# Value projection of a neighbourhood attention: every piece of side work tied to a numbered weight load

## The chip, the cores and the metric

The kernel runs on one NeuronCore of a Trainium2 chip. The metric is the device time of one execution, in microseconds (us). Five engines work side by side: TensorE (PE) multiplies matrices, VectorE (DVE) and ScalarE (ACT) work elementwise, GpSimd (POOL) does some elementwise work and issues DMAs, SyncE (SP) issues DMAs. Each takes its instructions in the order in which they were put into its program.

## The reference

One layer of a diffusion backbone over 256 latent tokens and 256 context tokens, 2048 channels each, in float32. Both are normalised and modulated to rows `h`. From `h` come the projections of a neighbourhood attention (16 heads of 64, here handled as 8 pairs of heads) and of a gated linear attention (GLA, 4 heads); both branches are gated, merged and projected out.

```python
h = _layer_norm(x) * (1.0 + scale) + shift
h_c = _layer_norm(ctx) * (1.0 + scale_c) + shift_c
aq, ak, av, az, bq, bk, bv, bz, bg, mga, mgb = _split_cols(h @ w_in[l])
y_a = _neighborhood_attention(heads(aq), heads(ak), heads(av), k_ctx, v_ctx, na_rpb[l])
y_b, y_b_c = _gla_mixer(bq, bk, bv, bg, ...)
out = _merge_branches(y_a, az, y_b, bz, mga, mgb, w_br_a[l], w_br_b[l], w_out[l])
```

A latent query attends, in one softmax, to a window of latent keys plus all context keys, with a bias table (`rpb`) on the window.

## The kernel before

All matrix products keep float32 precision by splitting each operand into a high and a low part and multiplying three times (high x high, high x low, low x high). The split of a weight is one cast on ACT (line 147, `h_...`) and one subtraction on DVE (line 149, `l_...`).

**Weight loads.** `load` (line 154) brings one unit of weights from HBM on SP's queue into a buffer `raw` (four of them), splits it into `hi` and `lo` (three of each), and the caller then multiplies with it. A weight unit is mostly 128 x 1024; in the value projection it is 128 x 704. The bias tables `rb` of the attention (line 475) use `raw` buffers too, and hold them until the scores have taken the bias. Counted from the first call of `load`: two units for the queries of each pair (`aq`, 48 matmuls of 256 columns for a pair), eight for each of the three groups of value columns (`av`, 24 matmuls of 352 columns per unit), two for the keys of pair 7 (`ak7`, 24 matmuls of 512 columns per unit), and then the GLA's keys and queries (`bk`, `bq`). The keys of pairs 0 to 6 are made earlier, in the first stage, with `h` itself.

**The order of the work.** The program text gives each instruction a place. A scheduler at compile time then puts each engine's instructions in order: among those that it expects to be ready, the earlier in the text goes first. `tc.issue_after(ins)` forces an instruction behind another one of the same engine. What the scheduler expects of durations is its own model; at run time the order is fixed, and an engine stands still at an instruction whose inputs are late.

**The stage.** The loop over `g` (line 555) projects the queries of pair 2g (`project_pair`), reads values for the pairs whose probabilities are ready (`read_values`, tile `op`), projects pair 2g+1, calls `attend` for both pairs and then `value_columns(g)`, the value projection (`va`). In the fourth round there are no value columns; `attend(6)` stands ahead of `project_pair(7)`, and the values of pair 7 are read by a hook in the GLA's first keys. `attend` works in two halves of 128 queries: scores of two heads on TensorE (tile `s`, one PSUM pair), bias and maximum on DVE (lines 485, 487), exponential on ACT (line 491), reciprocal and scaling (494 to 499), four transposes per head on TensorE (tile `tp`, line 502), copies into `pt` (506, 508). `project_pair` also splits the pair's keys (`kn`, `kl`) and moves them and parts of the queries across partitions by DMAs on POOL's queue (`kh` line 459, `q` line 470).

**The rows.** The GLA later reads `h` with tokens on the partitions. Since `h` was made transposed, eight blocks of rows are computed anew and stored in HBM (`hrows`). For a block n, `fetch_rows` issues three DMAs on POOL's queue: two broadcasts of the modulation (`sb`) and the input rows (`xr`). `store_rows` does four steps on DVE (lines 410, 411), splits the result over the two staging buffers themselves (`sb` takes the high part, `xr` the low one), stores them by four DMAs on POOL's queue (line 415), and fetches block n+1 into the same two buffers. `store_rows` is called after the second, fifth and eighth unit of a value group; the first DVE step is forced behind the last weight subtraction.

Of the kernel before, what the change touches and what calls it, by code (L numbers as in the profile page):

```python
# [88 lines left out]
def tile_backbone_layer(  # L89
# [46 lines left out]
    def bank(name):  # L136
        return ps.tile([P, 512], F32, tag="bank", name=name, bufs=2)
# [7 lines left out]
    def split(hi, lo, src, after=None):  # L145
        with tc.issue_after(after[0]) if after else nullcontext():
            cast = nc.scalar.copy(hi, src)  # L147
        with tc.issue_after(after[1]) if after else nullcontext():
            sub = nc.vector.tensor_tensor(out=lo, in0=src, in1=hi.bitcast(F32), op=ALU.subtract)  # L149
        return cast.ins, sub.ins  # L150

    subs = []

    def load(src, n, name, after=None):
        raw = stream.tile([P, 1024], F32, tag="raw", name=f"r_{name}", bufs=4)
        nc.sync.dma_start(raw[:, :n], src)
        hi = stream.tile([P, 1024], F32R, tag="hi", name=f"h_{name}")
        lo = stream.tile([P, 1024], F32R, tag="lo", name=f"l_{name}")
        subs.append(split(hi[:, :n], lo[:, :n], raw[:, :n], after)[1])
        return hi, lo  # L160

    def unit(name, k):
# [227 lines left out]
    def staging(shape, name, dt=F32R):  # L390
        return const.tile(shape, dt, tag="staging", name=name, bufs=2)

    staged = []

    def fetch_rows(n):
        s, cols = n // 4, slice(512 * (n % 4), 512 * (n % 4) + 512)
        sb, xr = staging([P, 2, 512], f"sb{n}"), staging([P, 2, 512], f"xr{n}")
        for m in range(2):
            nc.gpsimd.dma_start(sb[:, m, :].bitcast(F32), mods[m, s, cols].partition_broadcast(P))
        nc.gpsimd.dma_start(xr[:].bitcast(F32), xin[2 * s : 2 * s + 2, :, cols].rearrange("i p c -> p i c"))  # L400
        staged.append((n, sb, xr))

    def store_rows():
        n, sb, xr = staged.pop()
        b, f = sb[:].bitcast(F32), xr[:].bitcast(F32)
        s, c = n // 4, n % 4
        for i in range(2):
            x, j = f[:, i, :], 2 * s + i
            with tc.issue_after(subs[-1]):
                nc.vector.scalar_tensor_tensor(x, x, mvs[:, j, 0:1], b[:, 0, :], ALU.subtract, ALU.mult)  # L410
            nc.vector.scalar_tensor_tensor(x, x, rsn[:, 0, j : j + 1], b[:, 1, :], ALU.mult, ALU.add)
        split(sb[:], xr[:], f)
        for part, src in ((0, b), (1, f)):
            for i in range(2):
                nc.gpsimd.dma_start(
                    hrows[4 * c : 4 * c + 4, :, part, 2 * s + i, :].rearrange("f p c -> p f c"),
                    src[:, i, :].rearrange("p (f c) -> p f c", f=4),
                )
        if n + 1 < 8:
            fetch_rows(n + 1)  # L420

    store_modulation()
    fetch_rows(0)


    tri = k2([P, 2, P], "tri")
# [20 lines left out]
    def project_pair(p, q):  # L447
        kT = kTs[p // 4][:, p % 4, :]
        if p >= K0:
            kp = acc(f"kp{p}")  # L450
            project_t(f"ak{p}", kp[:], 512, hhi, hlo)
            nc.scalar.copy(kT, kp[:])
        kn = k2([P, 512], f"kn{p}", F32R)
        kl = k2([P, 512], f"kl{p}", F32R)
        split(kn[:], kl[:], kT)
        kh = k4([P, 2, 512], f"kh{p}", F32R)
        for j in range(2):
            for r, src in zip(half, (kn, kl)):
                nc.gpsimd.dma_start(kh[r, j, :], src[half[j], :])
        qp = acc(f"qp{p}")  # L460
        project_t(f"aq{p}", qp[:, :T], T, xh, xl)
        qh, ql = q[:, p % 2, 0], q[:, p % 2, 1]
        for j in range(2):
            r, o = half[j], half[1 - j]
            nc.scalar.mul(qh[r, j, :], qp[r, :T], 0.125)
            nc.vector.scalar_tensor_tensor(
                ql[r, j, :], qp[r, :T], 0.125, qh[r, j, :].bitcast(F32), ALU.mult, ALU.subtract
            )
            nc.scalar.mul(qh[o, j, :], qp[r, :T], 0.125)  # L469
            nc.gpsimd.dma_start(ql[o, j, :], ql[r, j, :])  # L470
        return qh, ql, kh

    def attend(p, qh, ql, kh):
        rt = stream.tile([P, 1024], F32, tag="raw", name=f"rb{p}", bufs=4)
        nc.sync.dma_start(rt[:, :768], rpb[p])
        rb = rt[:, :768].rearrange("p (j c) -> p j c", j=2)
        pt = k8([P, 2, 4, T], f"pt{p}")
        for qt in range(2):
            s2 = pair(f"s{p}_{qt}")
            for j in range(2):  # L480
                q = slice(P * qt, P * qt + P)
                mm(s2[:, j, :], qh[:, j, q], kh[:, j, :], True, False)
                mm(s2[:, j, :], ql[:, j, q], kh[:, j, :], False, True)
            o = P * (1 - qt)
            nc.vector.tensor_tensor(out=s2[:, :, :T], in0=s2[:, :, :T], in1=rb[:, :, o : o + T], op=ALU.add)
            nm = tiny([P, 2], "nm")
            nc.vector.tensor_reduce(nm[:], s2[:], AX.X, ALU.max, negate=True)
            pr = k4([P, 2, 512], f"pr{p}_{qt}")
            sm = tiny([P, 2], "sm")
            for j in range(2):  # L490
                nc.scalar.activation(
                    pr[:, j, :], s2[:, j, :], AF.Exp, bias=nm[:, j : j + 1], accum_out=sm[:, j : j + 1]
                )
            nc.vector.reciprocal(sm[:], sm[:])
            for j in range(2):
                if j:
                    nc.scalar.mul(pr[:, j, :], pr[:, j, :], sm[:, j : j + 1])
                else:
                    nc.vector.tensor_scalar(pr[:, j, :], pr[:, j, :], sm[:, j : j + 1], None, ALU.mult)
                tp = bank(f"tp{p}_{qt}_{j}")  # L500
                for kt in range(4):
                    nc.tensor.transpose(tp[:, P * kt : P * kt + P], pr[:, j, P * kt : P * kt + P], ident[:])
                dst = pt[:, j, :, P * qt : P * qt + P]
                src = tp[:].rearrange("p (k q) -> p k q", k=4)
                if j:
                    nc.vector.tensor_copy(dst, src)
                else:
                    nc.scalar.copy(dst, src)
        return pt

    def read_values(p):
        pt = probs.pop(p)
# [15 lines left out]
    def value_columns(g):  # L528
        va = [acc(f"va{g}_{t}") for t in range(4)]
        for k in range(0, KT, 2):  # L530
            wh, wl = load(wav[8 * g + k // 2], 2 * AVW, f"av{g}_{k}")
            project_rows([t[:, :AVW] for t in va], wh, wl, k, AVW, 4)
            if k in (2, 8, 14) and staged:
                store_rows()
        n = min(AVW, 1024 - AVW * g)
        for t in range(4):
            dst = vs[t // 2][:, t % 2, AVW * g : AVW * g + n]
            if t % 2:
                nc.vector.tensor_copy(dst, va[t][:, :n])
            else:  # L540
                nc.scalar.copy(dst, va[t][:, :n])
# [12 lines left out]

    probs, pairs = {}, {}
    for g in range(4):
        q = k8([P, 2, 2, 2, T], f"q{g}", F32R)
        pairs[2 * g] = project_pair(2 * g, q)
        for p in sorted(probs):
            read_values(p)  # L560
        if g == 3:
            probs[6] = attend(6, *pairs.pop(6))
        pairs[2 * g + 1] = project_pair(2 * g + 1, q)
        for p in sorted(pairs):
            probs[p] = attend(p, *pairs.pop(p))
        if g < 3:
            value_columns(g)
    read_values(6)


    cs = staging([P, 3, T], "cs", F32)
# [16 lines left out]
    hooks = [lambda: read_values(NP - 1)]  # L588

    def gates(h):  # L590
        zp = pair(f"z{h}")
# [198 lines left out]
        nc.vector.tensor_tensor(out=ya[:, p, :], in0=sg[:], in1=ya[:, p, :], op=ALU.mult)  # L790

    pws = [weights_of(0)]
    decays = gates(0)
    kq = keys(0), queries(0)
    parts = decayed(0, *decays, *kq)
    decays = gates(1)
    kq = keys(1), queries(1)
# [373 lines left out]
```

## Time and profile before

| what | value |
|---|---|
| median of three runs | 1268.09 us (1267.7 to 1273.63) |
| the profiled execution, its own time | 1272.22 us |
| its span, first to last instruction | 1270.5 us |
| TensorE busy | 1218.7 us (96%) |
| VectorE busy | 757.3 us (60%) |
| ScalarE busy | 538.0 us (42%) |
| GpSimd busy | 113.5 us (9%) |
| moved by DMA | 264.55 MB, mean 208 GB/s |

The profile is of one execution. Busy time of TensorE counts matmuls that overlap each other, so it is not work at full speed. Rows of a timeline give start, length, engine, line, operation, tiles, and in brackets the idle time before it and what ended it. Rows of waits give the total, the number and the longest. The chain of waits follows the last instruction back to what released it. A line such as L149 can be that of a helper used by many callers; the tile names tell them apart.

### The profile page before, as it was taken

What the parts mean: (1) busy time and instruction counts of PE and PEld (TensorE: products, weight loads), DVE (VectorE), ACT (ScalarE), POOL (GpSimd) and SP (SyncE); (2) the same over time, 40 slices, a digit from 0 to 9 for tenths busy, and PEclk for the clock granted to TensorE, in tenths of its full rate; (3) what the DMA queues carried; (4) which work ended last, traced back from release to release, by engine and by line L of the source; (5) the groups of instructions that cost most, each with busy time, mean ns of one, the idle gap of its engine ahead of it and who ended that gap; (6) DMA issues with size and microseconds to landing.
All of it is one profiled execution on the core that took longest, in us unless ns stands there. A gap on an engine that the chain in (4) does not pass through costs nothing.

```text
span 1270.5 us, 17135 instructions
## 1 busy us (share of the span) xinstructions
PE 1218.7 (96%) x6617; PEld 1020.8 (80%) x6617; DVE 757.3 (60%) x1094; ACT 538.0 (42%) x752; POOL 113.5 (9%) x162
## 2 busy tenths in 40 slices
PE   6999889798999999999999999999999999999997
PEld 5666688797878889888898898888888888888785
DVE  6655574656547756544642358987655554555677
ACT  4322454444435435334452364444434444445341
POOL 1000223242111101000100000000000000000112
PEclk9999989899999999999999999999999999999999
DMA  9996658595642424552545559998655555556661
GB/s 380 417 402 260 164 184 239 153 250 165 190 121 83 134 100 134 178 187 100 189 143 182 199 195 312 315 325 283 235 191 189 192 198 184 197 184 256 237 217 67
DMA packets 76706, 264.55 MB, mean 208 GB/s; under 512 B 9536, under 2 KB 10640, under 8 KB 71504
## 3 DMA queue, kind: packets, MB, share of 16 engines
q1 hardware_dynamic: 66464, 235.75, 53.8%
q0 software_dynamic: 9728, 27.15, 7.2%
q8 instruction: 52, 0.85, 0.3%
q10 hardware_dynamic: 432, 0.56, 0.1%
q14 instruction: 30, 0.25, 0.1%
HBM read 247.66 MB, written 10.52 MB: 203 GB/s over the span
## 4 chain that ended last, share of the span: by engine, by line
PE 66%; DMA 13%; DVE 11%; issue 6%; ACT 2%; POOL 1%; SPq 0%; DVEq 0%; ACTq 0%; POOLq 0%
PE mgb L143 7%; PE g L143 7%; PE pb L143 7%; PE o L143 7%; PE bk L143 7%; PE kp L143 7%; PE mga L143 5%; DMA wg<-in_wgate 4%; PE bq L143 4%; PE pa L143 3%; DMA xr<-in_xin 3%; PE wo L143 3%; PE az L143 2%; PE gp L143 2%; DVE l_bz L149 2%
## 5 line engine op out<-in xcount | busy, mean ns | idle before, releaser
L149 DVE TENSOR_TENSOR l_wv<-r_wv,h_wv 128x1024 fp32r<-128x1024 f32 x32 | 39.2, 1225 | 76.0 <-ACT h_wv L147 75.7
L143 PE MATMUL o<-h_wv,gt 128*128 128x512 f32 x256 | 83.7, 389 | 0.0
L143 PE MATMUL g<-ah,hr 128*128 128x512 f32 x256 | 79.0, 390 | 0.0
L149 DVE TENSOR_TENSOR l_pb<-r_pb,h_pb 128x1024 fp32r<-128x1024 f32 x32 | 39.2, 1225 | 47.8 <-ACT h_pb L147 47.8
L143 PE MATMUL va<-h_av,hhi 128*128 128x352 f32 x192 | 64.2, 334 | 0.6 <-ACT q L469 0.6
L143 PE MATMUL va<-l_av,hhi 128*128 128x352 f32 x192 | 64.3, 335 | 0.0
L143 PE MATMUL va<-h_av,hlo 128*128 128x352 f32 x192 | 64.1, 334 | 0.0
L147 ACT CAST h_wv<-r_wv 128x1024 fp32r<-128x1024 f32 x32 | 33.6, 1050 | 71.7 <-DMA r_wv<-in_wst 71.7
L149 DVE TENSOR_TENSOR l_mgb<-r_mgb,h_mgb 128x1024 fp32r<-128x1024 f32 x32 | 39.1, 1224 | 32.3 <-ACT h_mgb L147 32.3
L902 DVE SCALAR_TENSOR_TENSOR gacc<-wg,sc,gacc 128x512 f32<-128x512 f32 x64 | 46.5, 749 | 18.0 <-DMA wg<-in_wgate 17.6
L149 DVE TENSOR_TENSOR l_mga<-r_mga,h_mga 128x1024 fp32r<-128x1024 f32 x32 | 39.1, 1223 | 28.9 <-ACT h_mga L147 28.9
L143 PEld LDWEIGHTS o<-h_wv,gt 128*128 128x128 f32 x256 | 48.0, 188 | 10.0
L143 PEld LDWEIGHTS g<-ah,hr 128*128 128x128 f32 x256 | 47.8, 188 | 9.7
L143 PE MATMUL kp<-hhi,h_ak 128*128 128x512 f32 x128 | 52.8, 419 | 2.2 <-ACT hhi L301 2.2
L147 ACT CAST h_mga<-r_mga 128x1024 fp32r<-128x1024 f32 x32 | 33.7, 1055 | 49.1 <-PE mga L143 30.8
L147 ACT CAST h_mgb<-r_mgb 128x1024 fp32r<-128x1024 f32 x32 | 33.6, 1054 | 48.2 <-PE mgb L143 26.4
L147 ACT CAST h_pb<-r_pb 128x1024 fp32r<-128x1024 f32 x32 | 33.7, 1053 | 43.4 <-PE pb L143 30.1
L143 PE MATMUL kp<-hhi,l_ak 128*128 128x512 f32 x128 | 51.7, 404 | 0.0
L143 PE MATMUL bk<-hhi,h_bk 128*128 128x512 f32 x128 | 50.8, 397 | 0.7 <-ACT kf L624 0.7
L143 PE MATMUL kp<-hlo,h_ak 128*128 128x512 f32 x128 | 50.7, 398 | 0.0
L301 ACT ACTIVATE hhi<-xt,mds 128x256 fp32r<-128x256 f32 x32 | 17.5, 594 | 78.1 <-DVE mds L295 78.1
L143 PE MATMUL bk<-hlo,h_bk 128*128 128x512 f32 x128 | 50.4, 394 | 0.0
(355 smaller groups left out, 3616.5 us busy)
## 6 DMA issues: line engine op xcount, KB each, us to landing
wm<-in_wmod SPq DMA_DIRECT2D x32, 1024.0 KB, 9.4
hr<-hrows SPq DMA_DIRECT2D x32, 512.0 KB, 4.3
r_wv<-in_wst SPq DMA_DIRECT2D x32, 512.0 KB, 3.6
r_bz<-in_wst SPq DMA_DIRECT2D x32, 512.0 KB, 4.7
wg<-in_wgate SPq DMA_DIRECT2D x64, 256.0 KB, 5.3
r_mga<-in_wst SPq DMA_DIRECT2D x32, 512.0 KB, 3.3
r_mgb<-in_wst SPq DMA_DIRECT2D x32, 512.0 KB, 3.3
r_pb<-in_wst SPq DMA_DIRECT2D x32, 512.0 KB, 3.3
```

Source lines behind the costliest of these rows:

```text
L143: return nc.tensor.matmul(o, a, b, start=start, stop=stop).ins
L147: cast = nc.scalar.copy(hi, src)
L149: sub = nc.vector.tensor_tensor(out=lo, in0=src, in1=hi.bitcast(F32), op=ALU.subtract)
L301: cast = nc.scalar.activation(hhi[:, s, kt, :], x, AF.Identity, scale=m, bias=b)
L902: nc.vector.scalar_tensor_tensor(part, raw[:], sc[:, n // 4, 0:1], part, ALU.mult, ALU.add)
```

## The change

`load` now keeps a list of the cast and subtraction of every load, and a table `events` from a load's number to calls that it makes right after that load's split, before the caller's matmuls.

- The eight blocks of rows become three events each: at load 6+5n the three row loads, now on SP's queue and forced behind that load's own DMA, and the four DVE steps, forced behind its subtraction; at load 7+5n the split, into one `hi` and one `lo` buffer of the weights' three; at load 12+5n the four stores, on SP's queue and forced behind that load's DMA. The two staging buffers hold only `sb` and `xr`.
- `attend` becomes `attention`, which gives back two calls, scores and transposes (`turns`). In a value group whose first load has number n, the scores stand at loads n+1, n+3, n+5, n+7, the transposes at n+3, n+5, n+7, n+9, and the reading of both pairs' values at n+12. Both pairs' queries are projected ahead of the group.
- Pairs 6 and 7 get places in the same manner, among the loads of `ak7`, `aq7` and of the GLA's first keys and queries; the hook goes.
- The split of the keys of pairs 2 and up is forced behind the cast and subtraction of the last load but one.
- The GLA's `keys(0)` is called ahead of `gates(0)`.

No arithmetic is added or left out.

```diff
     def load(src, n, name, after=None):
         raw = stream.tile([P, 1024], F32, tag="raw", name=f"r_{name}", bufs=4)
-        nc.sync.dma_start(raw[:, :n], src)
+        dma = nc.sync.dma_start(raw[:, :n], src).ins
         hi = stream.tile([P, 1024], F32R, tag="hi", name=f"h_{name}")
         lo = stream.tile([P, 1024], F32R, tag="lo", name=f"l_{name}")
-        subs.append(split(hi[:, :n], lo[:, :n], raw[:, :n], after)[1])
+        cast, sub = split(hi[:, :n], lo[:, :n], raw[:, :n], after)
+        loads.append((cast, sub))
+        for event in events.pop(len(loads), ()):
+            event(dma, sub)
         return hi, lo
...
+        def fetch_and_scale(dma, sub):
+            sb, xr = staging([P, 2, 512], f"sb{n}", F32), staging([P, 2, 512], f"xr{n}", F32)
+            with tc.issue_after(dma):
+                for m in range(2):
+                    nc.sync.dma_start(sb[:, m, :], mods[m, s, cols].partition_broadcast(P))
+                nc.sync.dma_start(xr[:], xin[2 * s : 2 * s + 2, :, cols].rearrange("i p c -> p i c"))
+            for i in range(2):
+                x, j = xr[:, i, :], 2 * s + i
+                with tc.issue_after(sub):
+                    nc.vector.scalar_tensor_tensor(x, x, mvs[:, j, 0:1], sb[:, 0, :], ALU.subtract, ALU.mult)
+                nc.vector.scalar_tensor_tensor(x, x, rsn[:, 0, j : j + 1], sb[:, 1, :], ALU.mult, ALU.add)
+            tiles["x"] = xr
+
+        def parts(dma, sub):
+            hi = stream.tile([P, 2, 512], F32R, tag="hi", name=f"hr{n}")
+            lo = stream.tile([P, 2, 512], F32R, tag="lo", name=f"lr{n}")
+            with tc.issue_after(sub):
+                split(hi[:], lo[:], tiles["x"][:])
+            tiles["hi"], tiles["lo"] = hi, lo
+
+        def store(dma, sub):
+            with tc.issue_after(dma):
+                for part, key in enumerate(("hi", "lo")):
+                    for i in range(2):
+                        nc.sync.dma_start(
+                            hrows[4 * c : 4 * c + 4, :, part, 2 * s + i, :].rearrange("f p c -> p f c"),
+                            tiles[key][:, i, :].bitcast(F32).rearrange("p (f c) -> p f c", f=4),
+                        )
...
+    for n in range(8):
+        for step, event in zip((0, 1, 6), rows_of_h(n)):
+            events.setdefault(len(loads) + 6 + 5 * n + step, []).append(event)
...
-        split(kn[:], kl[:], kT)
+        split(kn[:], kl[:], kT, loads[-2] if p >= 2 else None)
...
-            if k in (2, 8, 14) and staged:
-                store_rows()
...
+    for g in range(3):
         q = k8([P, 2, 2, 2, T], f"q{g}", F32R)
+        first, second = project_pair(2 * g, q), project_pair(2 * g + 1, q)
+        s0, t0 = attention(2 * g, *first)
+        s1, t1 = attention(2 * g + 1, *second)
+        n = len(loads) + 1
+        at(n + 1, (s0, 0))
+        at(n + 3, (s0, 1), (t0, 0))
+        at(n + 5, (s1, 0), (t0, 1))
+        at(n + 7, (s1, 1), (t1, 0))
+        at(n + 9, (t1, 1))
+        at(n + 12, (read_values, 2 * g), (read_values, 2 * g + 1))
+        value_columns(g)
+    q = k8([P, 2, 2, 2, T], "q3", F32R)
+    first = project_pair(6, q)
+    s0, t0 = attention(6, *first)
+    n = len(loads)
+    at(n + 2, (s0, 0))
+    at(n + 4, (s0, 1), (t0, 0))
+    second = project_pair(7, q)
+    s1, t1 = attention(7, *second)
+    at(n + 6, (s1, 0), (t0, 1))
+    at(n + 8, (s1, 1), (t1, 0), (read_values, 6))
+    at(n + 10, (t1, 1))
+    at(n + 12, (read_values, 7))
...
     pws = [weights_of(0)]
+    kf = keys(0)
     decays = gates(0)
-    kq = keys(0), queries(0)
+    kq = kf, queries(0)
```

More of the change, by code (lines that the diff above doesn't have):

```diff
@@ L150, in split @@
         return cast.ins, sub.ins
-    subs = []
+    loads, events = [], {}
     def load(src, n, name, after=None):
         raw = stream.tile([P, 1024], F32, tag="raw", name=f"r_{name}", bufs=4)
-        nc.sync.dma_start(raw[:, :n], src)
+        dma = nc.sync.dma_start(raw[:, :n], src).ins
         hi = stream.tile([P, 1024], F32R, tag="hi", name=f"h_{name}")
         lo = stream.tile([P, 1024], F32R, tag="lo", name=f"l_{name}")
-        subs.append(split(hi[:, :n], lo[:, :n], raw[:, :n], after)[1])
+        cast, sub = split(hi[:, :n], lo[:, :n], raw[:, :n], after)
+        loads.append((cast, sub))
+        for event in events.pop(len(loads), ()):
+            event(dma, sub)
         return hi, lo
@@ L391, in staging @@
         return const.tile(shape, dt, tag="staging", name=name, bufs=2)
[L393 to L401, printed above, removed]
@@ L403, in store_rows, with rows_of_h @@
-    def store_rows():
-        n, sb, xr = staged.pop()
-        b, f = sb[:].bitcast(F32), xr[:].bitcast(F32)
-        s, c = n // 4, n % 4
[L407 to L413, printed above, removed]
-            for i in range(2):
[L415 to L420, printed above, removed]
+    def rows_of_h(n):
+        s, c = n // 4, n % 4
+        cols = slice(512 * c, 512 * c + 512)
+        tiles = {}
+        def fetch_and_scale(dma, sub):
[4 more added lines that the diff above has]
+                nc.sync.dma_start(xr[:], xin[2 * s : 2 * s + 2, :, cols].rearrange("i p c -> p i c"))
+            for i in range(2):
+                x, j = xr[:, i, :], 2 * s + i
[17 more added lines that the diff above has]
+                        )
+        return fetch_and_scale, parts, store
@@ L422, in tile_backbone_layer @@
+    for n in range(8):
+        for step, event in zip((0, 1, 6), rows_of_h(n)):
+            events.setdefault(len(loads) + 6 + 5 * n + step, []).append(event)
     store_modulation()
-    fetch_rows(0)
     tri = k2([P, 2, P], "tri")
@@ L471, in project_pair, with attention @@
         return qh, ql, kh
-    def attend(p, qh, ql, kh):
+    def attention(p, qh, ql, kh):
         rt = stream.tile([P, 1024], F32, tag="raw", name=f"rb{p}", bufs=4)
@@ L477, in attend, with scores @@
         pt = k8([P, 2, 4, T], f"pt{p}")
-        for qt in range(2):
+        weights = {}
+        def scores(qt):
             s2 = pair(f"s{p}_{qt}")
@@ L499, in attend, with turns @@
                     nc.vector.tensor_scalar(pr[:, j, :], pr[:, j, :], sm[:, j : j + 1], None, ALU.mult)
+            weights[qt] = pr
+        def turns(qt):
+            pr = weights.pop(qt)
+            for j in range(2):
                 tp = bank(f"tp{p}_{qt}_{j}")
@@ L508, in attend, with at @@
                     nc.scalar.copy(dst, src)
-        return pt
+        probs[p] = pt
+        return scores, turns
+    def at(step, *calls):
+        for fn, *args in calls:
+            events.setdefault(step, []).append(lambda *_, fn=fn, args=args: fn(*args))
     def read_values(p):
@@ L553, in value_columns @@
                 nc.vector.tensor_tensor(out=lr[r, :], in0=lp[r, :], in1=lr[r, :].bitcast(F32), op=ALU.subtract)
-    probs, pairs = {}, {}
-    for g in range(4):
+    probs = {}
+    for g in range(3):
         q = k8([P, 2, 2, 2, T], f"q{g}", F32R)
[L558 to L568, printed above, removed]
+        first, second = project_pair(2 * g, q), project_pair(2 * g + 1, q)
[21 more added lines that the diff above has]
+    at(n + 12, (read_values, 7))
     cs = staging([P, 3, T], "cs", F32)
@@ L586, in rope_of @@
         eng.tensor_tensor(out=dst[:], in0=dst[:], in1=t[:], op=ALU.add)
-    hooks = [lambda: read_values(NP - 1)]
+    hooks = []
     def gates(h):
```

## The prediction, on record before the changed kernel ran

> **What bounds the kernel now.** I read the slices of the page first, then the table of windows, the waits of TensorE (PE), the waits of VectorE (DVE), and then the chain and the timelines around single stalls.
>
> ```profile
> PE   6999889798999999999999999999999999999997
> ```
>
> The kernel is bound by TensorE: from slice 11 to slice 39 the row has 9 everywhere. The digits below 9 behind the start-up lie in slices 5 to 10 (31.8 us each), inside the stage that the change rebuilds. Two windows compare it with the stage behind it.
>
> ```profile
> core 0: us, PE busy (x) PEld busy (x) DVE busy (x) ACT busy (x) POOL busy (x), PEclk, DMA share, GB/s
> 141.30:397.00 255.70, 226.22 (x1398) 203.42 (x1396) 144.07 (x215) 113.77 (x207) 62.62 (x102) 0.93 0.63 182
> 397.00:500.00 103.00, 103.00 (x639) 93.27 (x638) 72.68 (x135) 48.32 (x69) 15.11 (x15) 1.00 0.36 119
> ```
>
> From 141.3 to 397 us TensorE has a granted clock of 0.93 and sits idle; behind it the clock is 1.00 and nothing is idle. DVE is busy 144 of 256 us and ACT 114, so neither is full. Busy time overstates what matmuls need, since they overlap, so I build the stage's floor from start-to-start rates of undisturbed runs.
>
> ```profile
> 214.80 3.60 PE op L143 x32
> ...
> 404.89 11.51 PE bq L143 x96
> 416.86 21.78 PE bk L143 x96
> ```
>
> ```profile
> 237.87 6.87 DMA xr<-in_xin
> ...
> 250.04 2.08 PE s L143 x4
> ...
> 259.36 1.04 PE tp L502 x8
> 260.40 12.27 PE va L143 x77
> ```
>
> These are chain rows: start, length, what, count. A value matmul (352 columns) costs 12.27/77 = 0.159 us, one of 256 columns 11.51/96 = 0.120, one of 512 columns 21.78/96 = 0.227, a transpose 1.04/8 = 0.13, a matmul of the value reading 3.60/32 = 0.113. The code asks in this stage for 3 x 8 x 24 = 576 value matmuls (91.6 us), 8 x 48 = 384 of the query projection (46.1), 64 scores (14.5), 48 of the key projection of pair 7 and some 63 of `bk`, all of 512 columns (25.2), 128 transposes (16.6; neighbours hide part, I take 14.5), 128 records of value reading (14.5) and about 1.2 us of small ones. Floor: 207.6 us. The stage takes 255.7, so **48 us are lost in it**, and that is all that this change can win.
>
> Where they go is in the waits of TensorE in that window: total, times, longest.
>
> ```profile
> PE s L143 <- ACT pr L491: 16.4, 3, 6.9
> PE s L143 <- DMA q<-q: 4.5, 5, 1.8
> PE qp L143 <- ACT v L541: 3.1, 2, 2.3
> PE s L143 <- DMA kh<-kl: 2.4, 1, 2.4
> PE s L143 <- ACT q L469: 2.3, 1, 2.3
> PE va L143 <- ACT q L469: 0.6, 1, 0.6
> ```
>
> That is 29.3 us of idling; the other 48 - 29.3 = 18.8 us are matmuls at a lower clock behind the stalls:
>
> ```profile
> 374.15 0.47 PE L143 MATMUL s<-kh,q 128*128 128x512 f32 x1 [2.42 <-DMA kh<-kl]
> ...
> 375.63 0.63 PE L143 MATMUL bk<-hhi,h_bk 128*128 128x512 f32 x1
> 376.05 0.63 PE L143 MATMUL bk<-hhi,l_bk 128*128 128x512 f32 x1
> ```
>
> Two neighbours start 0.42 us apart where the undisturbed rate is 0.227: nearly half speed, after a stall of only 2.4 us. So I count a stall of 2 us with a slow sequel.
>
> **Who holds the scores up.** The three longest waits name ACT's exponentials, which wait for DVE, and DVE waits for row data:
>
> ```profile
> DVE xr L410 <- DMA xr<-in_xin: 28.5, 5, 7.2
> ```
>
> ```profile
> 153.33 0.69 DVE L149 TENSOR_TENSOR kl<-kT,kn 128x512 fp32r<-128x512 f32 x1 [6.63 <-DMA kh<-kn]
> ...
> 244.76 0.75 DVE L410 SCALAR_TENSOR_TENSOR xr<-xr,mvs,sb 128x512 f32<-128x512 f32 x1 [7.23 <-DMA xr<-in_xin]
> ```
>
> At 244.76 DVE has stood 7.23 us in front of a row step whose data are not there; the maximum of the scores is queued behind it, ACT waits for that, and TensorE starts its next scores at 250.04. The row load was issued only at 237.87, because its buffer was freed by the stores of the row before. At 153.33 DVE stands 6.63 us for a buffer needed by keys of pair 2, work that is not yet due, with the queries of pair 0 queued behind it.
>
> **The change, part by part.**
>
> *Row loads on SP, far ahead.* The arithmetic of a row is the same (four steps, a cast, a subtraction); only its place changes. Row n is loaded right behind weight load 6+5n on SP's queue, scaled behind that load's subtraction, split one load later, and stored from SP at load 12+5n. There are four weight buffers, so load L is issued when the subtraction of load L-4 is done; where two bias tiles (`rb`) hold buffers it is L-2. A value unit is 24 x 0.159 = 3.8 us, so the lead is 7.6 to 15 us. What must arrive in it:
>
> ```profile
> r_av<-in_wav SPq DMA_DIRECT2D x24, 352.0 KB, 5.8
> ...
> xr<-in_xin POOLq DMA_DIRECT2D x8, 512.0 KB, 7.2
> hrows<-sb POOLq DMA_DIRECT2D x16, 256.0 KB, 3.2
> hrows<-xr POOLq DMA_DIRECT2D x16, 256.0 KB, 4.2
> ```
>
> Issue to landing is 7.2 us for a row, about 1.5 us more for its three issues: some 8.7 us. It fits at four and three buffers of lead and is late by about 1 us at two, which concerns rows 0, 3 and 5. The waits on rows cost 16.4 + 3.1 = 19.5 us of idling (the `qp` waits stem from ACT standing at a row's cast). I leave 3 us of it.
>
> *Issue cost on SP.* Seven DMAs for each of eight rows come to SP. No row shows such a store issued there; the nearest are these:
>
> ```profile
> 254.27 1.49 POOL L415 DMA_DIRECT2D hrows<-xr  x2 [0.72 <-DVE xr L149]
> ```
>
> ```profile
> 322.55 0.33 SPq L475 DMA_DIRECT2D rb<-in_rpb  x1
> ```
>
> Between 0.33 and 0.75 us each, 56 DMAs take 18 to 42 us of SP over 200 us, where SP stands waiting anyway:
>
> ```profile
> SPq L156 <- DVE l_av L149: 100.4, 23, 11.4
> ```
>
> So I cost the issues at nothing; the cover is those 100 us. Without it a store group would delay the next weight load by 4 x 0.75 = 3 us. On POOL's side 56 issues fall away, and its own moves of `kh` and `q` no longer queue behind rows.
>
> *The order of keys.* `split(kn, kl)` of pairs 2 and up is tied behind an earlier load's operations. The 6.63 us stop before the first scores goes. Load 5, issued at about the same time as row 0 before, no longer shares the DMA engines with it. Value unit 5 now stands before the first scores and covers their queries. The first stall is 2.3 us (`q` by ACT) plus 0.9 + 1.8 = 2.7 us of the `q<-q` waits; I leave 1.5 of 5.0.
>
> *Scores and transposes at fixed units.* From scores to their transposes there are two value units, 7.6 us. The work between them, undisturbed, runs from the second row of this fence to the second row of the next (the first rows are a weight's subtraction and cast):
>
> ```profile
> 231.25 0.88 DVE L149 TENSOR_TENSOR l_av<-r_av,h_av 128x704 fp32r<-128x704 f32 x1
> 232.05 0.69 DVE L485 TENSOR_TENSOR s<-s,rb 128x512 f32<-128x512 f32 x1
> ```
>
> ```profile
> 235.84 0.78 ACT L147 CAST h_av<-r_av 128x704 fp32r<-128x704 f32 x1
> 236.50 0.73 ACT L497 ACTIVATE pr<-pr,sm 128x512 f32<-128x512 f32 x1
> ```
>
> From 232.05 to 237.23 is 5.2 us, about 6 with the scores' own end. 1.6 us remain for other work on DVE, more than one weight subtraction, less than the four steps of a row (3.0 us): at a row I expect stalls of up to 1 us.
>
> *Pairs 6 and 7.* Their scores now stand behind a unit of 24 x 0.227 = 5.4 us or more. The stalls there are what is left of the waits, 1.8 + 2.4 + 0.6 = 4.8 us; the chain over POOL is a little longer than one unit, so I leave 2.
>
> *The new wait.* Row parts no longer use the row's own buffers but one of three `hi` and `lo` weight buffers, from the split until the stores have landed. For most of the stage weights have two. Then the cast of load L can start only when TensorE has ended unit L-2, and has one unit, 3.8 us, for a cast and a subtraction (0.78 + 0.88 = 1.7 us, about 1.9 with the handovers). Behind a delayed subtraction stand the softmax steps on DVE. From below it costs nothing; from above, 1 us in each of some 24 value units. I take 2 us, near the lower end, since DVE is busy only 56% of the time.
>
> *Clock.* With the long stalls gone, of 18.8 us I leave 4, for the short ones that stay; the 0.63 us rows at 375 are my reason to leave anything. The Trainium skill (TensorE: Matmul & The Clock Gate, "What's actually happening") has the clock halved only after an idle window of about 3.4 us. By that rule stalls of 1 or 2 us would cost no clock and the sum below would end 4 us lower, at 1229 us; the stall of 2.42 us in this trace was followed by half speed all the same, which is why I go by the row.
>
> Sum of what stays: 3 + 1.5 + 2 + 2 + 4 = 12.5 us. Gain: 48 - 12.5 = 35.5 us. The span would be 1270.5 - 35.5 = 1235.0, and the profiled execution's own time 1272.22 - 35.5 = 1236.7. That execution lies 4.1 us over the median of 1268.09, so against the median the sum is 1232.6: **I predict 1233 us.**
>
> **The rivals.**
>
> *Rows still late.* The lead counts for little, because the row's megabyte and the weights share the same DMA engines (share 0.63 in this stage) and now the same queue, so a weight load behind a row waits for it. For it: the last piece of the row alone took 6.87 us from 237.87. Against it: that load had no lead at all, and now has two units or more. If every second row stalls TensorE by 2.5 us with 1 us of slow clock, 4 x 3.5 = 14 us come back: 1247 us. The Trainium skill (DMA: Bandwidth & Descriptors, "Issuing engines are not separate DMA queues") says that another issuing engine saves only issue time. By that rule SP's queue lands a row no sooner than POOL's did, and 1247 us is what follows if the lead alone falls short; no row load on SP is in this trace.
>
> *The order does not follow.* The unit numbers set only priorities; if TensorE's order stays nearly as it is and only the rows come earlier, the 19.5 us and half of the slow clock go, less the 3 and 2 us: 24 us, 1244 us.
>
> *The third buffer decides (slower).* If weight casts are given the buffer of a row before its stores have landed, ACT stands at that cast with the exponentials behind it. Place: each row's stores, which stand on SP behind a weight load. Price: load 5.8, issues 3.0, store 4.2 us = 13.0, less two units of 7.6, gives 5.4 us, and 2.5 us of slow clock (18.8 us over some eight stalls now): 7.9 x 8 = 63 us against the 35.5: 1295 us. It decides once a store lands over two units behind its split. Against it: load and store overlap mostly.
>
> *Stalls change places.* With two weight buffers and 3 us row steps in one unit the lost time stays near 48 us: 1266 us.
>
> **How the numbers follow.** Forecast 0.62 (1222 to 1243), rows late 0.15, order 0.11, stalls change places 0.05, third buffer 0.07. The range starts at the floor, 1268 - 48 = 1220, and ends at 1257, ten over the late rows; beyond lie the last two rivals and little of the others. A measurement can tell 0.5% (6.3 us) from no change: faster 0.88, same 0.05, slower 0.07.
>
> **What would show it.** Right: the wait of `xr` for its load falls from 28.5 us to under 6, no stall of scores over 3 us, the stage ends near 361 us with a clock of at least 0.97, the rest unchanged. Wrong: waits of ACT's `h_av` or of row parts for `hrows` stores, value matmuls waiting for `l_av`, or SP standing in front of stores.

## The result, and the profile after

| | before | after |
|---|---|---|
| median | 1268.78 us (1267.7 to 1273.63, 4 runs) | 1250.89 us (1246.56 to 1252.66, 4 runs) |
| ratio | | 0.985, 95% interval 0.981 to 0.988 |
| profiled execution, its span | 1270.5 us | 1251.0 us |
| mean granted clock over the span | 0.985 | 0.991 |

The change gains 18 us, 1.5%, about half of the 35 us that were forecast. I compare the traces in the order of the prediction. First the slices of TensorE on the page of the kernel after, where a slice is 31.3 us:

```profile
PE   6999999989899999999999999999999999999997
```

Before, slices 5, 6, 8 and 10 were below 9, one of them a 7. Now two are, 9 and 11, with an 8 each: the same stage still has holes. The table of windows (us, busy time of each engine with its instructions, granted clock, DMA share, GB/s) puts a size to it:

```profile
core 0: us, PE busy (x) PEld busy (x) DVE busy (x) ACT busy (x) POOL busy (x), PEclk, DMA share, GB/s
141.30:378.00 236.70, 220.77 (x1388) 201.89 (x1387) 142.50 (x212) 111.19 (x204) 25.35 (x49) 0.96 0.68 197
397.00:500.00 103.00, 102.28 (x636) 92.65 (x636) 70.97 (x151) 47.80 (x72) 12.48 (x13) 1.00 0.35 114
```

Before, TensorE was idle for 30 of 256 us here with a clock of 0.93; now it is idle for 16 of 237 us with 0.96. Behind the stage nothing has changed. All that was won lies in the stage: TensorE starts the 96th matmul of the GLA's first queries at 416.12 us before and at 396.81 after, 19.3 us sooner, and the span is 19.5 us shorter.

To compare kernels whose instructions stand in different orders I use one yardstick for all: the time from the first query matmul of pair 0 to the start of that 96th `bq` matmul. It holds the same products in all of them. By the prediction's rates its floor is 226.6 us: the 207.6 us of the sum, 33 more `bk` (7.5) and 96 `bq` (11.5). Before it takes 274.8 us, so 48.2 are lost; after 255.5, so **28.9 us are still lost**, where the forecast left 12.5.

The waits of TensorE from 136 to 400 us (total, times, longest) show that the old ones went and others came:

```profile
PE qp L143 <- ACT v L565: 4.1, 1, 4.1
PE s L143 <- DMA q<-q: 3.8, 3, 2.8
PE va L143 <- ACT q L482: 2.9, 2, 2.3
PE lp L572 <- ACT v L565: 2.2, 1, 2.2
...
PE va L143 <- DVE l_av L149: 0.5, 1, 0.5
```

The scores' waits for exponentials (16.4 us before) are gone. All rows of the stage come to 15.8 us where there were 29.3. The two longest rows that name `v` on ACT need a look at ACT and DVE. On DVE the row data are in time now, and a new kind of wait has come:

```profile
DVE l_av L149 <- DMA hrows<-lr: 3.6, 1, 3.6
DVE xr L410 <- DMA xr<-in_xin: 2.9, 1, 2.9
...
DVE lr L149 <- DMA hrows<-lr: 1.4, 1, 1.4
```

```profile
ACT h_av L147 <- DMA hrows<-hr: 9.3, 3, 4.8
ACT h_av L147 <- DMA hrows<-lr: 7.5, 1, 7.5
...
ACT h_aq L147 <- DMA hrows<-lr: 2.2, 1, 2.2
...
ACT hr L147 <- DMA hrows<-hr: 0.3, 1, 0.3
```

The wait of `xr` fell from 28.5 us to 2.9, once, for row 0. In its place casts on ACT and subtractions on DVE stand 24.3 us in front of stores of rows, a wait that before did not have. All but 1.7 us of it (the `hr` and `lr` rows, a row's own split) are splits of weights: they were given a buffer out of which a row was still being stored.

The worst stall of TensorE shows how this reaches it. (The other row that names `v`, 2.2 us at 314.57, comes behind a cast that stood 4.8 us for a store until 303.19, but with row steps in between the trace does not close that chain.) The chain of waits (start, length, what):

```profile
242.56 0.33 SPq L156
...
242.93 7.76 DMA hrows<-hr
250.69 2.24 issue
252.93 0.23 ACT h_aq L147
253.15 0.72 issue
253.88 0.45 ACT v L565
...
254.37 4.63 PE qp L143 x24
```

and ACT's timeline at the same place:

```profile
246.14 0.58 ACT L528 COPY pt<-tp 128x512 f32<-128x512 f32 x1
252.93 1.04 ACT L147 CAST h_aq<-r_aq 128x1024 fp32r<-128x1024 f32 x1 [6.21 <-issue]
253.88 0.45 ACT L565 COPY v<-va 128x352 f32<-128x352 f32 x1
254.22 0.69 ACT L506 ACTIVATE pr<-s,nm 128x512 f32<-128x512 f32 x1
```

SP issues a weight load and right behind it the stores of a row, at 242.93. ACT comes after 246.7 to the cast of an earlier load. Those weights were issued at 236.91 and have been there since 240.61, but the cast has been given the row's buffer and stands 6.2 us. The first store of `hr` lands at 250.69. The list names nothing for the 2.24 us behind that; the landing events in the trace have the second store of `hr` at 252.86, 0.07 us before the cast starts. So this stall is one for stores too, and comes on top of the 24.3 us. TensorE had been done with the last value unit, and so with another of the three buffers, since 250.3. Behind the cast, in ACT's order, stand a copy of values out of PSUM and the exponentials. TensorE needs the PSUM of that copy and stands 4.1 us until 254.37; then 24 query matmuls take 4.63 us where 24 undisturbed ones take 2.9 (24 x 0.120), so the clock costs another 1.7.

### The profile page after: what moved, and what is told of

The parts are those of the page before. It is cut to its first block, busy times and chain, and to the rows that moved or that the text cites. A ratio compares the mean times of both kernels' runs of the same rounds, so it can differ in the third digit from the quotient of the medians.

```text
span 1251.0 us, 17120 instructions
## 1 busy us (share of the span) xinstructions
PE 1212.5 (97%) x6617; PEld 1018.8 (81%) x6617; DVE 753.5 (60%) x1094; ACT 536.9 (43%) x752; POOL 73.7 (6%) x106
## 4 chain that ended last, share of the span: by engine, by line
PE 75%; DVE 8%; DMA 8%; issue 4%; ACT 2%; SPq 1%; POOL 1%; DVEq 0%; POOLq 0%; ACTq 0%
PE g L143 7%; PE mgb L143 7%; PE mga L143 7%; PE pb L143 7%; PE o L143 7%; PE bk L143 7%; PE kp L143 6%; PE va L143 5%; PE bq L143 4%; PE pa L143 3%; PE wo L143 3%; DMA wg<-in_wgate 2%; PE az L143 2%; PE gp L143 2%; PE qp L143 2%
## 5 line engine op out<-in xcount | busy, mean ns | idle before, releaser
L143 PE MATMUL bz<-l_bz,hhi 128*128 128x512 f32 x128 | 50.2, 392 | 1.0 <-DVE l_bz L149 1.0
L143 PE MATMUL bk<-hhi,l_bk 128*128 128x512 f32 x128 | 50.7, 396 | 0.0
```

The source lines that it names most:

```text
L143: return nc.tensor.matmul(o, a, b, start=start, stop=stop).ins
```

## The experiments

My theory after this (A): what is missing was taken by the row parts in the weights' buffers, whose stores land late. The rivals: the fixed order did all of the work (B), the loads and DVE steps of the rows cost what is left, on SP's queue, on the DMA engines or on DVE (C), or the new order has stalls of its own (D). Each ratio is to executions of before timed along with that kernel (medians 1266.2 to 1266.9 us, for after 1268.78). Stage times and waits below are from one profiled execution each, which can lie some us off the median (pool_stores 1243.31, in_place 1237.06); "lost" is the stage less 226.6 us, "rest" is the span less the end of the stage.

| kernel | median us | ratio to before, 95% | stage | lost | rest |
|---|---|---|---|---|---|
| before | 1268.78 | | 274.8 | 48.2 | 854.4 |
| after | 1250.89 | 0.981 to 0.988 | 255.5 | 28.9 | 854.2 |
| order_only | 1258.19 | 0.991 to 0.995 | 262.6 | 36.0 | 854.1 |
| rows_only | 1257.06 | 0.990 to 0.994 | 263.2 | 36.6 | 852.4 |
| pool_stores | 1247.26 | 0.981 to 0.988 | 248.2 | 21.6 | 852.2 |
| two_rows | 1231.17 | 0.969 to 0.973 | 236.0 | 9.4 | 852.1 |
| two_stores | 1234.17 | 0.972 to 0.980 | 236.7 | 10.1 | 853.1 |
| in_place | 1234.04 | 0.971 to 0.977 | 237.2 | 10.6 | 856.8 |
| in_place_pool | 1238.57 | 0.975 to 0.980 | 240.6 | 14.0 | 853.7 |
| two_plus_one | 1270.38 | 1.001 to 1.005 | 240.9 | 14.3 | 889.5 |
| in_place_8 | 1244.29 | 0.979 to 0.984 | 238.9 | 12.3 | 862.0 |
| kl_free | 1248.86 | 0.982 to 0.989 | 251.3 | 24.7 | 852.4 |
| kl_only | 1268.58 | 0.999 to 1.002 | 271.5 | 44.9 | 852.3 |
| store_at_5 | 1250.85 | 0.984 to 0.990 | 258.1 | 31.5 | 852.5 |

**order_only: the new order, with the rows as they were.** `fetch_rows` and `store_rows` of the kernel before are back.

```diff
-    for n in range(8):
-        for step, event in zip((0, 1, 6), rows_of_h(n)):
-            events.setdefault(len(loads) + 6 + 5 * n + step, []).append(event)
...
+            if k in (2, 8, 14) and staged:
+                store_rows()
```

> The rows as before (loads and stores on POOL's queue, parts in the staging buffers, fetched when the block before is stored), scores, transposes and key splits at the new places. Theory A (the late rows were most of the old loss, the order a smaller part): DVE still waits over 15 us in all for xr, and the time is 1257 to 1264 us. Rival B (the fixed order did the work): the waits on xr no longer reach TensorE and the time is that of the changed kernel, 1251 us within 4.

Measured 1258.19 us. The row data are still late, on DVE:

```profile
DVE xr L413 <- DMA xr<-in_xin: 19.6, 5, 8.0
```

Yet only 36.0 us are lost, and TensorE idles 21.2 us in the stage where before it idled 29.3: the units put between the scores and whoever waits for them absorb part of the late rows. The order alone is worth 0.7%.

**rows_only: the new rows, in the order of before.** The tie of the keys and the earlier `keys(0)` are out too.

```diff
-    for g in range(3):
...
-        first, second = project_pair(2 * g, q), project_pair(2 * g + 1, q)
-        s0, t0 = attention(2 * g, *first)
...
+    for g in range(4):
...
+        pairs[2 * g] = project_pair(2 * g, q)
+        for p in sorted(probs):
+            read_values(p)
```

> The rows at their new places (loads and stores on SP, parts in the weights' hi and lo buffers), scores and transposes in the old order and the key split free. Theory A: the waits on xr fall under 6 us, the first stall of some 5 us and the stalls of pairs 6 and 7 stay, the casts that wait for row stores stay: 1254 to 1262 us. Rival B: without the fixed order nothing is gained, 1264 to 1270 us.

Measured 1257.06 us, 0.8%. The wait for row data is down to 3.7 us, and in its place come the waits for stores, of which this one on ACT is the largest:

```profile
ACT h_av L147 <- DMA hrows<-hr: 16.2, 4, 9.2
```

All rows of this kind come to 38.7 us. So 28.5 us of one wait were exchanged for more of another, and the halves (0.7% and 0.8%) add up to the 1.5% of the whole.

**pool_stores: the four stores of a row issued by POOL, with no forced place.**

```diff
         def store(dma, sub):
-            with tc.issue_after(dma):
+            with nullcontext():
...
-                        nc.sync.dma_start(
+                        nc.gpsimd.dma_start(
```

> The changed kernel with the four stores of a block on POOL's queue, free to go as soon as the split is done. Theory A (what is left of the loss comes from weight casts that wait for a row's buffer until its stores, queued on SP behind a weight load, have landed): the stores land in 3 to 5 us instead of 7, the casts' waits on hrows fall from some 19 us to under 6, and the time is 1238 to 1246 us. Rival C (the stores' place does not matter; the rest is DVE work and shared DMA engines): 1251 us within 4.

Measured 1247.26 us (1243.31 to 1250.94), not told apart from after. The stores do land sooner, as the list of DMA issues shows (count, KB, median us to landing), first after, then this kernel:

```profile
hrows<-hr SPq DMA_DIRECT2D x16, 256.0 KB, 7.0
hrows<-lr SPq DMA_DIRECT2D x16, 256.0 KB, 7.0
```

```profile
hrows<-hr POOLq DMA_DIRECT2D x16, 256.0 KB, 3.3
hrows<-lr POOLq DMA_DIRECT2D x16, 256.0 KB, 4.2
```

but casts and subtractions still wait 24.8 us for them (10.6 + 2.4 on ACT, 9.0 + 2.8 on DVE), and DVE's wait for `xr` is 11.7 us where after has 2.9. (The 21.6 us of the table are from the fastest of its four executions, 1243.31.) In this form theory A fell: it is not the late landing alone. A buffer that serves a row for a cast, a subtraction and a store is missing to the weights even when the store is quick.

**two_rows: the ceiling.** Only blocks 0 and 4 are computed and stored, and the GLA reads these in place of the others.

```diff
-    for n in range(8):
+    for n in (0, 4):
...
-            nc.sync.dma_start(hr[:].bitcast(F32), hrows[f])
+            nc.sync.dma_start(hr[:].bitcast(F32), hrows[f % 4])
```

> The changed kernel with two of the eight row blocks kept; the other six are neither loaded, computed nor stored, and the GLA reads the two blocks in their place, so the output is another one. It gives the ceiling of the new order without most of the row work. Theory A: most of the 28 us that are still lost in the stage go, 1230 to 1238 us. Rival D (the new order itself leaves the stalls): 1244 to 1251 us.

Measured 1231.17 us, 9.4 lost. With three quarters of the row work gone the stage comes within 10 us of the floor, so the new order is no obstacle, and no run comes below the floor of the prediction.

**two_stores: all eight blocks loaded, computed and split as after, only two of them stored.**

```diff
-                    for i in range(2):
+                    for i in range(2 if c == 0 else 0):
...
-            nc.sync.dma_start(hr[:].bitcast(F32), hrows[f])
+            nc.sync.dma_start(hr[:].bitcast(F32), hrows[f % 4])
```

> The changed kernel with all eight row blocks loaded, scaled and split, but only two of them stored (the GLA reads those two in place of all, so the output is another one). Six of eight times the hi and lo buffer of a row comes free as soon as it is split. Theory A (hold of the third buffer and the stores cost what is left): near the kernel with two blocks, 1231 to 1238 us. Rival C (the rows' DVE steps and loads cost it): 1243 to 1251 us.

Measured 1234.17 us, 10.1 lost, 0.7 more than with the row arithmetic left out. Loads, DVE steps, casts and the parts in the weights' buffers all remain, and cost next to nothing. What costs is that a buffer stays taken until a store has landed (and what the stores do to the queue, which two_plus_one parts from it).

**in_place: the parts over the row's own staging buffers, as before, stores by POOL one load after the split.** The weights keep all three `hi` and `lo`; row loads stay on SP, places and order as after.

```diff
-            hi = stream.tile([P, 2, 512], F32R, tag="hi", name=f"hr{n}")
-            lo = stream.tile([P, 2, 512], F32R, tag="lo", name=f"lr{n}")
             with tc.issue_after(sub):
-                split(hi[:], lo[:], tiles["x"][:])
+                split(tiles["hi"][:], tiles["lo"][:], tiles["lo"][:].bitcast(F32))
...
-            with tc.issue_after(dma):
+            with nullcontext():
...
-                        nc.sync.dma_start(
+                        nc.gpsimd.dma_start(
...
-        for step, event in zip((0, 1, 6), rows_of_h(n)):
+        for step, event in zip((0, 1, 2), rows_of_h(n)):
```

> The changed kernel with the row's parts written over its own two staging buffers, as before the change, so that weights keep all three hi and lo buffers; stores on POOL's queue behind the split, row loads on SP at the same units. Theory A: no cast waits for hrows any more and the time falls by 8 to 15 us under the changed kernel, 1236 to 1243 us; SP may stand for the staging buffers until the stores have landed. Rival C: 1247 to 1253 us.

Measured 1234.04 us (1231.48 to 1237.06), the fastest kernel with all the work in it: 2.6% below before, and 17 us below after by the medians (some 14 by the two ratios, 0.974 and 0.985). No cast waits for a store. Its window, and its longest waits of TensorE from 136 to 400 us (6.4 us in all in the stage):

```profile
141.30:378.00 236.70, 230.26 (x1522) 212.19 (x1521) 156.62 (x236) 122.08 (x219) 54.51 (x86) 0.99 0.68 205
```

```profile
PE va L143 <- ACT q L480: 2.5, 1, 2.5
PE s L143 <- DMA q<-q: 2.5, 3, 1.1
PE s L143 <- ACT pr L504: 1.2, 1, 1.2
```

The row's buffers are now held from load to store again, as before. That did not bring the late rows back: with the lead of the new places DVE waits 6.9 us for rows in total where before it waited 28.5.

**in_place_pool: the same, row loads on POOL's queue too.**

```diff
-            with tc.issue_after(dma):
+            with nullcontext():
                 for m in range(2):
-                    nc.sync.dma_start(b[:, m, :], mods[m, s, cols].partition_broadcast(P))
+                    nc.gpsimd.dma_start(b[:, m, :], mods[m, s, cols].partition_broadcast(P))
```

> The same with the row loads on POOL's queue too, the units unchanged: SP carries weights and bias tables alone. If SP's queue for the loads matters (a row is early because it is queued behind its weight load), DVE waits for xr again, over 10 us in all, and the time is 1246 to 1256 us. If only the early place matters, it is within 3 us of the kernel with loads on SP.

Measured 1238.57 us. The queue of the loads and their forced place, one of the parts of the change, are worth 4.5 us by the medians at most: the ranges 1231.48 to 1237.06 and 1237.22 to 1241.44 just miss each other, but the intervals of the ratios overlap. DVE waits 8.6 us for `xr`, against 6.9 in in_place and 28.5 before, so most of the cure for late rows is the early place.

**two_plus_one: buffers parted the other way.** Weights get two `hi` and `lo` in the whole kernel, row parts one of their own; stores stay on SP.

```diff
-        hi = stream.tile([P, 1024], F32R, tag="hi", name=f"h_{name}")
+        hi = stream.tile([P, 1024], F32R, tag="hi", name=f"h_{name}", bufs=2)
...
-            hi = stream.tile([P, 2, 512], F32R, tag="hi", name=f"hr{n}")
+            hi = stream.tile([P, 2, 512], F32R, tag="hrow", name=f"hr{n}", bufs=1)
```

> The changed kernel with the three hi and lo buffers divided in the text: two for weights everywhere, one for rows alone. No weight cast can be put into a row's buffer; the stores stay on SP. Theory A, if it is the assignment of a row's buffer to a weight that costs: 1243 to 1249 us, less whatever two buffers cost in the later stages. If it is having only two buffers that costs: 1251 to 1262 us, with value matmuls waiting for l_av.

Measured 1270.38 us, no gain at all, and still the most telling run. In the stage only 14.3 us are lost, with the slow stores on SP unchanged (they land in 7.4 us here). All of the loss lies behind it, where the rest takes 889.5 us in place of 854.2. TensorE's window there, this kernel and then before:

```profile
400.00:1200.00 800.00, 786.61 (x3806) 658.71 (x3805) 450.96 (x580) 340.07 (x422) 28.62 (x28) 1.00 0.57 198
```

```profile
420.00:1200.00 780.00, 776.57 (x3816) 657.31 (x3815) 454.91 (x607) 341.83 (x426) 28.60 (x29) 1.00 0.59 201
```

It is idle for 13 us where it was idle for 3. From the 96th `bq` matmul to the end TensorE waits 29 us in all, against 6 in after. Of these, 18.7 us name casts and subtractions of splits; the longest single wait stands at the very end, where before had 1.8 us:

```profile
PE y L143 <- DVE dn L1111: 9.6, 1, 9.6
```

So two buffers are enough for the weights of this stage, and not for those behind it; how they lead to that last wait the runs do not show. A third set for the weights beside one for the rows was not run.

**in_place_8: rows two loads later,** to keep row 0 off the first scores.

```diff
-            events.setdefault(len(loads) + 6 + 5 * n + step, []).append(event)
+            events.setdefault(len(loads) + 8 + 5 * n + step, []).append(event)
```

> The kernel with row parts in place, all row units two loads later (8+5n), so that the first block's four steps no longer stand on DVE in front of the queries of pair 1. If the first stall (2.5 us of idling and its slow sequel) comes from those steps, the time falls by 2 to 4 us under 1234, to 1230 to 1232 us. If it comes from the load of the weights or the moves of q over POOL, it stays at 1234 within 2.

Measured 1244.29 us, a miss. The first stall did go, but a `q<-q` wait of 4.6 us came at 319.58. And the last row ends so late that it holds up the GLA: its four steps on DVE start only at 581.96, in front of the GLA's tiles `near`, and its stores land at 591.43, where in in_place they land at 328.12. Waits of TensorE from 500 to 760 us:

```profile
PE ap L143 <- DVE near L714: 5.0, 2, 3.0
PE g L143 <- DMA hr<-hrows: 1.7, 1, 1.7
```

In in_place neither wait is there. The rest takes 862.0 us against 856.8.

**kl_free and kl_only: the tie of the keys,** taken out of after, and put into before alone.

```diff
-        split(kn[:], kl[:], kT, loads[-2] if p >= 2 else None)
+        split(kn[:], kl[:], kT)
```

> The changed kernel without the tie of the key split to an earlier load. If the tie removed the stop of 6.6 us in front of the first scores, that stop is back and the time is 1254 to 1259 us; if the fixed order alone did that, it stays at 1251 within 3.

> The kernel before with nothing but that tie. If the tie is worth the first stall by itself, 5 us of idling and some slow clock go: 1259 to 1263 us against 1267. If not, the kernel before, within 3.

Measured 1248.86 and 1268.58 us, the same as after and as before. In kl_free the stop ahead of the first scores does not come back. In kl_only the key split no longer stands there, but DVE stands nearly as long at the same place, now in front of a weight's subtraction:

```profile
153.98 0.89 DVE L149 TENSOR_TENSOR l_av<-r_av,h_av 128x704 fp32r<-128x704 f32 x1 [5.88 <-ACT h_av L147]
```

TensorE starts its first scores at 154.40 us, where before it started them at 155.24.

**store_at_5: stores one load earlier,** ahead of the next row's loads on SP.

```diff
-        for step, event in zip((0, 1, 6), rows_of_h(n)):
+        for step, event in zip((0, 1, 5), rows_of_h(n)):
```

> The changed kernel with the stores one load earlier on SP (11+5n instead of 12+5n), in front of the next block's loads. If a weight cast is put into a row's buffer wherever the compile-time order thinks the stores done, the casts still wait for hrows by some 20 us and the time stays at 1251 within 5. If the length of the hold decides, it falls to 1238 to 1245 us.

Measured 1250.85 us, as after. The stores land sooner, from the same queue:

```profile
hrows<-hr SPq DMA_DIRECT2D x16, 256.0 KB, 4.6
hrows<-lr SPq DMA_DIRECT2D x16, 256.0 KB, 5.0
```

Yet the waits for stores fall only a little, from 24.3 to 21.3 us, and the late rows are back behind the stores in the queue: DVE waits 24.0 us for `xr`. The two effects are not parted. Under shared buffers none of the three places of the stores that I tried (after, pool_stores, this one) is free.

## Why the prediction was half right

**Right.** The stage, and it alone, set the gain. Its floor holds: two_rows, two_stores and in_place come to within 9 to 11 us of it. Late rows were one cause, and they are gone (2.9 us of DVE's wait left of 28.5; I had left 3 of the 19.5 that reached TensorE). The order was worth about as much as the rows. Of my signs of being right, the wait of `xr`, the stalls of scores (2.8 us at most) and the unchanged rest came; the early end of the stage and a clock of 0.97 did not, and the first sign of being wrong, casts waiting for `hrows` stores, did. An arrangement whose new waits cost almost nothing, as my sum had them, gives 1234 us as in_place, but by other means: there weights and rows share no buffer. The time measured, 1250.89, lies inside the range of 1220 to 1257 by luck: the range reached that far for late rows, which did not come.

**Where it failed: "The new wait. ... I take 2 us".** I saw the wait and named its sign, casts in front of `hrows` stores, but sized it by the wrong bound. I asked whether two buffers give a cast time enough: yes, 3.8 us for 1.7. Two_plus_one bears that out. But the rows do not leave the weights two buffers in rotation. Which buffer a cast gets is settled when the program is built, so a cast that is assigned the row's buffer stands until the stores have landed, even when another is free by then, as in the stall above, and on ACT everything behind it stands too. The measured size, with its slow clock, is **14.6 us** (28.9 - 14.3) by two_plus_one, where nothing but the buffers differs from after, and 18.3 us (28.9 - 10.6) by in_place, which also moves the stores to POOL and closer behind the split. The sum was 16.4 us short (28.9 against 12.5), and 12.6 to 16.3 of them are this one term. The rival "the third buffer decides" had the right mechanism and place, at 63 us. It charged every row with 5.4 us and its slow sequel; in the trace the waits are 24.3 us in all, of 7.5 at the longest, with the 6.2 us of the stall above on top, and only a few of them reach TensorE. My reason against it, that load and store overlap, holds and does not help: the load issued at 242.56 lands at 249.98 and the stores behind it at 250.69 to 253.83, but it is an earlier load's cast, its weights long there, that stands for those stores.

**"So I cost the issues at nothing".** Not so on SP, where the two timelines differ. SP's timeline of after:

```profile
242.56 0.33 SPq L156 DMA_DIRECT2D r_aq<-in_wst  x1
242.93 1.15 SPq L425 DMA_DIRECT2D hrows<-hr  x2
244.12 2.76 SPq L425 DMA_DIRECT2D hrows<-lr  x2
246.98 2.86 SPq L156 DMA_DIRECT2D r_aq<-in_wst  x1
```

Four stores take 3.9 us to issue, not 1.3 to 3.0, more than the 3 us I named as the price without cover. The weight load behind them takes 2.86 us where the one ahead took 0.33, but the list of SP's waits puts 2.6 us of that down to DVE, so how far the stores delay it stays open. How much of all this reaches TensorE by itself the runs bound loosely: in two_plus_one it is still there, and the stage loses 3.7 us more than in_place.

**"Clock ... I leave 4".** It follows the stalls. After, 28.9 us lost less 15.8 idle leaves 13.1 for slower matmuls and small gaps; in in_place 10.6 - 6.4 = 4.2. By the granted clock in the traces, half speed lasts 20.5 us of the stage in after and 3.4 in in_place, which costs at most half of that, 10.2 and 1.7 us. The term was right for the stalls that I had assumed and too small for those that came.

**"I leave 1.5 of 5.0" and "I leave 2".** Under-sized, but small: the first stall is 2.3 us and a slow sequel, as row 0 keeps DVE from the queries; pairs 6 and 7 keep most of 3.8 us of `q<-q`.

**"The 6.63 us stop before the first scores goes".** It goes, but not by the tie that I gave it to. With the new order the tie is worth nothing (kl_free), and without the order it is worth nothing either (kl_only).

## What to carry to other kernels

Before a side task borrows from a rotating set of buffers, look up how long it holds one, to the landing of its last DMA, and which instruction is given that buffer next: that instruction, and all behind it on its in-order engine, inherit the wait; faster stores alone did not cure it here (24.8 us of waits against 24.3). Overwriting the side task's own buffers keeps its delays to itself, if its place in the order gives it a lead. Number the places of moved work in loads, but test each shift: two loads later cost 10 us by the medians here, in part because the last row then ended right in front of the work that reads it.

## What the runs showed of the hardware

**A queue changes the size of the pieces.** The same 32 stores, on SP in after and on POOL in pool_stores; the DMA lines from 136 to 400 us:

```profile
DMA packets 34315, 50.21 MB, mean 190 GB/s; under 512 B 2688, under 2 KB 20160, under 8 KB 34296
```

```profile
DMA packets 20120, 50.73 MB, mean 192 GB/s; under 512 B 2704, under 2 KB 3792, under 8 KB 20100
```

The counts run on: each takes in the ones before it. From SP there are some 16,400 more packets of 512 bytes to 2 KB and some 2,200 fewer larger ones. By the packets' sizes in the traces, a store of 256 KB goes out from SP as 512 pieces of 512 bytes, the length of one run in HBM, and from POOL as 64 pieces of 4 KB. The stores took 7.0 us to land from SP where from POOL they took 3.3 and 4.2. The landing goes with the place more than with the pieces: in store_at_5, from SP with the same pieces but ahead of the next row's loads, they took 4.6 and 5.0 us, and in in_place, from POOL, 4.3 and 4.7. The Trainium skill (DMA: Bandwidth & Descriptors, "Issuing engines are not separate DMA queues") has another issuing engine save only issue time. These last two kernels agree with that: 0.3 us lie between them.

**Half speed can come late.** TensorE's timeline of after, behind a stall of 2.21 us:

```profile
314.57 0.30 PE L572 MATMUL lp<-ident,lt 128*128 128x128 f32 x1 [2.21 <-ACT v L565]
...
315.43 0.28 PE L143 MATMUL qp<-hhi,h_aq 128*128 128x256 f32 x1
315.54 0.28 PE L143 MATMUL qp<-hhi,l_aq 128*128 128x256 f32 x1
...
316.88 0.41 PE L143 MATMUL qp<-hlo,h_aq 128*128 128x256 f32 x1
317.10 0.41 PE L143 MATMUL qp<-hhi,h_aq 128*128 128x256 f32 x1
```

The windows before and behind the switch (columns as above):

```profile
312.60:316.00 3.40, 1.43 (x12) 1.46 (x13) 2.82 (x14) 3.31 (x7) 0.00 (x0) 1.00 0.36 131
316.00:319.40 3.40, 3.40 (x18) 3.40 (x17) 1.62 (x5) 0.18 (x2) 0.00 (x0) 0.50 0.31 87
```

The first query matmuls start 0.12 us apart, full speed; from 316 us they start 0.21 apart, with a granted clock of 0.50, and at 319.4 the clock is back. So a stall of 2.2 us is paid twice, the second time over 3.4 us of work that begins 1.4 us later and looks undisturbed by any wait. The longer stalls, 4.1 us at 254 and 2.3 us at 160, are followed by half speed at once.

The granted clock shows when the switch can come: in the stage of after, half speed starts at 158.98, 254.56, 316.00 and 356.95 us, that is 28, 18 and 12 times 3.413 us apart, and lasts 3.41 or 6.83 us. The switches of this trace fall on a grid of 3.41 us, and the stall that ended at 314.57 is paid for from the next point of the grid on. The length of a stall alone does not decide: in kl_free the same wait of 2.21 us, at 312.61, has no sequel, while one of 2.17 us there has, and in kl_only one of 3.22 us has none. In in_place a stall of 1.2 us (the `s <- ACT pr` row) has none. The Trainium skill (TensorE: Matmul & The Clock Gate, "What's actually happening") has the clock halved after an idle window of about 3.4 us and released after as long a busy one. The length of the slow stretch agrees; a whole idle window was not needed, since in the 3.40 us before 316.00 TensorE was busy for 1.43.
